# Two fixed small experts open both tracks, in place of one fixed big expert, in a mixture-of-experts block

## The chip, the cores and the metric

The kernel runs on one core of one Trainium2 chip. The metric is the time of one execution on the device in microseconds (us); lower is better. The engines are named as in the profile: PE (matmul) with PEld (its weight loads), DVE (vector), ACT (scalar), POOL, and SP, whose queue issues most DMAs. PEclk is the granted clock of PE, 1.00 being 2.4 GHz and 0.50 being 1.2 GHz.

## The reference, cut to what matters

One layer on 512 tokens of width 1024: a pooling mixer and a latent attention, an output projection, then a mixture of experts with 32 experts, of which each token takes 4, and a final norm. The change touches the experts alone:

```python
logits = (ht @ w_router + b_router).astype(jnp.float32)
top_vals, top_idx = lax.top_k(logits, TOP_K)          # TOP_K = 4 of 32
gates = jax.nn.softmax(top_vals, axis=-1)
...
gu = xblk @ w_gate_up[e] + b_gate_up[e]               # 1024 -> 2048
gate = jnp.minimum(gu[:, :D_EXPERT], SWIGLU_LIMIT)
up = jnp.clip(gu[:, D_EXPERT:], -SWIGLU_LIMIT, SWIGLU_LIMIT)
act = gate * jax.nn.sigmoid(SWIGLU_ALPHA * gate) * (up + 1)
return act @ w_down[e] + b_down[e]                    # 1024 -> 1024
```

All is float32. The weights of an expert are 12 MB: 8 MB for gate and up, 4 MB for down. Router and inputs are fixed by the reference; worked out from it, the experts get 22 to 116 tokens, 12 of them more than 64 (67, 68, 76, 76, 80, 95, 98, 100, 114, 114, 115, 116), and experts 0 and 1 get 58 and 48.

## The kernel before, in words

Until about 200 us the kernel does the attention part, then the second norm and the router. After that it works through 32 positions, one expert each. Which expert stands at a position is decided on the chip: `ordering()` (L1235) ranks the experts by their counts, so that the fullest stand at the big positions. `KINDS` (L40) says what a position is:

- A **big** position (B) holds up to 128 tokens. Its weights are split into two float32r parts (`mhi` on ACT, `mlo` on DVE or POOL, L921 and L922), and each product is three matmuls (`mm3`, L98). 144 matmuls of 128x512 in all: 96 for gate and up, 48 for down.
- A **small** position (S) holds up to 64 tokens and multiplies the float32 weights unsplit, with two 64-column halves of the array side by side. 48 matmuls, each of which the trace shows as two records: 8 records for each MB of weights.

An expert is cut into 12 **items** of 1 MB of weights: gate and up 0 to 7 ("gu"), down 0 to 3 ("dn"). The big experts and the last small one form the x track (results in the psum banks tagged x), the other small ones the y track; `interleave` (L1353) merges both into one `plan` of 384 items, and PE runs it in order. Below, B0gu0 is item gu 0 of the big expert at position 0. Each item has one load of 1 MB into one of 9 slots (`load_slot`, L787), which SP issues in a fixed order; a slot is free again when its item's split or its matmuls are done. A load of an expert that is routed needs the expert's number, `eid` (L1260, read at L1432), which `ordering()` gives. SP also reads `nov` (L1555), the number of experts that overflow their position; it stands in the middle of the loads.

For a routed expert, its tokens are found by `select` (one-hot tiles `oh`, L841 and L843), `slot_info` (matmuls `m<-aux,oh`, L911, and columns `sl`), `fetch` (an indirect DMA of the rows, `xr`, L866) and `gather` (PE transposes `m<-ident,xr`; results in `xgh` and `xgl` for a big expert, in `xgs` for two small ones). After gate and up come the activation, its transposes (`m<-ident,au`), down, and later `combine` (L1106), which adds an expert's rows, or those of a pair of small ones, to `y`.

Position 0 is always expert 0, as a big one: its mask is known early (`mask0`, L658), its rows come straight from matmuls with `oh0` (tile `rows`, L701), its weights need no `eid`, and its eight gate-and-up items run on PE while the routing (`ordering()` and what follows, called by `opening()`, L1485) runs on DVE, PE and ACT. Only then can the first routed expert, S1, start.

Of the kernel before, what the change touches and what calls it, by code (L numbers as in the profile page):

```python
# [39 lines left out]
KINDS = "BSSS" + "BS" * 12 + "SSSS"  # L40
NBIG = KINDS.count("B")

assert len(KINDS) == 32 and KINDS[0] == "B" and KINDS.endswith("SS") and NBIG % 2 == 1
# [7 lines left out]
TURN, SHORT = 0.2, 3.0  # L51
FILL1 = 2
# [70 lines left out]
def block_kernel(ctx: ExitStack, tc: tile.TileContext, xT, x, pos, vecs, w_in, w_pool, w_qb, w_kvb, w_out,  # L123
# [67 lines left out]
    G.memset(keyadd[:, 0:1], BOOST)  # L191
# [46 lines left out]
    dma(br, b_router.partition_broadcast(P))  # L238

# [363 lines left out]
    mask0 = cst.tile([P, NT, 1], BF16, name="mask0")  # L603
    pos0 = cst.tile([P, NT], F32, name="pos0")
# [46 lines left out]
    def choose(a, b, src):  # L651
# [6 lines left out]
        V.tensor_tensor(mask0[:, a:b, :], logits[:, a:b, 0:1], mx[:, a:b, 3:4], op=ALU.is_ge)  # L658
# [27 lines left out]
    def first_slots(tt):  # L686
        a, b = tt[0], tt[-1] + 1
        pw = pt("pw0", bufs=5)
        places(pw, mask0, tt)
        V.scalar_tensor_tensor(pos0[:, a:b], pw[:, a:b], 1.0, mask0[:, a:b, 0], op0=ALU.add, op1=ALU.mult)  # L690
        for t in tt:
            V.tensor_scalar(oh0[:, t, :], iota_s, pos0[:, t:t + 1], None, op0=ALU.is_equal)
# [127 lines left out]
    load_gate_up(0, load_expert(0, 0))  # L820
    load_down(0, wdown[0], range(2))

# [8 lines left out]
    def onx(r):  # L831

        return big(r) or r == E - 1
# [14 lines left out]
    def mate(r):  # L848

        q = next((q for q in range(r + 1, E) if not big(q)), None)  # L850
        return q
# [18 lines left out]
    def gather(r):  # L870
# [66 lines left out]
    def biases(r, cs, first=True):  # L937
        for c in cs:
            bs = bias[:, c * T:(c + 1) * T]
            if big(r):  # L940
                PE.matmul(banks[r][c], lhsT=m4b[0:96, r:r + 1].to_broadcast([96, P]), rhs=bs, start=first,
                          stop=not first)
            else:
                q = 64 * (c % 2)
                PE.matmul(banks[r][c // 2][q:q + 64, :], lhsT=m4b[0:96, r:r + 1].to_broadcast([96, 64]), rhs=bs,
                          start=True, stop=False)

    def gate_up(r, k):


        first = r == 0 or r == "o"
        if k == 0:
            banks[r] = [bank("x" if onx(r) else "y") for _ in range(4 if big(r) else 2)]
        if big(r):
# [4 lines left out]
            for n, (hf, c) in enumerate(todo):  # L959
                cs = slice(c * T, (c + 1) * T)  # L960
                if k == 0 and not first:
                    biases(r, [2 * hf + c])
                mm3(PE, banks[r][2 * hf + c], xg[r][0][:, k, :], xg[r][1][:, k, :], parts[hf][0][:, cs],
                    parts[hf][1][:, cs], first and k == 0, r != 0 and k == KD - 1)
                if n == 1:
                    yield
        else:
            w = wslots.pop((r, "gu", k))
            for c in range(4):
                q = 64 * (c % 2)  # L970
                if k == 0 and c % 2 == 0:
                    biases(r, [c, c + 1])
                PE.matmul(banks[r][c // 2][q:q + 64, :], lhsT=xg[r][:, k, :], rhs=w[:, c * T:(c + 1) * T],
                          start=False, stop=(k == KD - 1))
        if r == 0 and k == KD - 1:
            biases(0, range(4), False)
# [42 lines left out]

    def down(r, j):  # L1020

        if j == 0:
            banks[r] = [bank("x") for _ in range(2)] if big(r) else [bank("y")]
# [26 lines left out]
        else:  # L1050
# [11 lines left out]
            if par == 0:  # L1062
                yb["s"] = (mo.tile([P, 2, T], F32R, tag="ysh", bufs=1, name="ysh"),
                           mo.tile([P, 2, T], F32R, tag="ysl", bufs=1, name="ysl"))
                scat["s"] = [mo.tile([P, T], F32R, tag=f"ss{c}", bufs=1, name=f"ss{c}") for c in range(2)]
            yh, yl = yb["s"]
            places = [(slice(64 * q, 64 * q + 64), q ^ par) for q in range(2)]
            for ps_, c in places:
# [100 lines left out]
    onehot[0] = oh0  # L1169
# [47 lines left out]
    bd = mo.tile([96, D], F32R, tag="ysh", bufs=1, name="bd")  # L1217
    bdraw = [mo.tile([96, T], F32, tag=tag, bufs=n, name="bdraw") for tag, n in (("xgs", 2), ("ats", 1))]
# [10 lines left out]
    gT = mo.tile([96, T], F32R, tag="ss1", bufs=1, name="gT")  # L1229
# [5 lines left out]
    def ordering():  # L1235
# [4 lines left out]
        V.tensor_scalar(keyc, cn[:, E:E + 1], float(E), col(C_KEY), op0=ALU.mult, op1=ALU.add)  # L1240
# [20 lines left out]
        pgp = bank("y")  # L1261
# [5 lines left out]
        pgo = bank("y")  # L1267
# [25 lines left out]
        V.tensor_scalar(capc, rank, float(NBIG), 64.0, op0=ALU.is_lt, op1=ALU.mult)  # L1293
        V.tensor_scalar(capc, capc, 64.0, None, op0=ALU.add)
# [9 lines left out]
        stp = bank("y")  # L1304
# [23 lines left out]
        ovs = bank("y")  # L1328
# [320 lines left out]
```

## Time and profile before

| | |
|---|---|
| time, median of 3 runs (lowest to highest) | 1296.73 us (1294.97 to 1298.3) |
| the profiled execution: its time, its span | 1297.45 us, 1295.4 us |
| mean granted clock of PE | 0.974 |
| busy: PE, DVE, ACT, POOL | 95%, 69%, 44%, 25% |
| a load of 1 MB of gate and up, from issue to landing, median | 9.3 us |
| moved from memory | 430.24 MB, of which 403 MB are the experts' weights |

The span runs from the first to the last instruction; some 2 us of the time lie outside it. Busy shares are averages over stages, and a busy PE may still run at half its clock, so the stretches are read one by one.

### The profile page before, as it was taken

How to read it: one execution, taken by the hardware profiler on the slowest of the kernel's cores; microseconds unless marked ns; L12 is line 12 of the kernel's file. 1: busy time of each engine (PE TensorE's matmuls, PEld its weight loads, DVE VectorE, ACT ScalarE, POOL GpSimd, SP SyncE). 2: the span in 40 equal slices, each digit the busy share in tenths (PEclk: the TensorE clock that was granted, in tenths of full speed). 3: DMA queues.
4: the chain of work that ended last, by engine and by line, in shares of the span. 5: the costliest groups of instructions: out<-in, count | busy, mean ns of one | idle time of the engine just before them, and what ended most of it. 6: DMA issues, size and time to landing. Idle time of an engine off the chain costs nothing.

```text
span 1295.4 us, 16730 instructions
## 1 busy us (share of the span) xinstructions
PE 1230.3 (95%) x5657; PEld 723.6 (56%) x5657; DVE 892.0 (69%) x1568; ACT 571.0 (44%) x819; POOL 319.2 (25%) x262
## 2 busy tenths in 40 slices
PE   7979986799989999999999999999999999999995
PEld 6856765556445555554555555465565555555432
DVE  6897676856767768665776867567677767667424
ACT  5467643444433545443454444345245444443213
POOL 2355452312211122121212113122121312221001
PEclk9999996799999999999999999999999999999998
DMA  8212324889979999999999999999999999999991
GB/s 315 90 50 94 134 82 166 290 319 361 398 318 360 428 415 415 387 405 427 379 408 404 388 384 405 397 367 372 408 406 391 375 425 399 405 424 390 399 406 68
DMA packets 86994, 435.71 MB, mean 336 GB/s; under 512 B 9239, under 2 KB 9239, under 8 KB 54136
## 3 DMA queue, kind: packets, MB, share of 16 engines
q1 hardware_dynamic: 82818, 420.43, 81.1%
q0 software_dynamic: 3888, 13.76, 2.8%
q8 instruction: 46, 0.75, 0.2%
q10 hardware_dynamic: 198, 0.39, 0.1%
q14 instruction: 44, 0.36, 0.1%
HBM read 430.24 MB, written 4.33 MB: 335 GB/s over the span
## 4 chain that ended last, share of the span: by engine, by line
PE 84%; DVE 10%; ACT 2%; issue 2%; DMA 2%; POOL 0%; SPq 0%; DVEq 0%; ACTq 0%; POOLq 0%
PE x L115 32%; PE y L115 30%; PE m L115 11%; PE acc L115 3%; DVE mlo L922 3%; PE po L115 3%; PE s L115 1%; PE pa L115 1%; ACT mhi L921 1%; DMA bdraw<-in_b_down_dram 1%; PE pp L115 1%; DVE oh L843 1%; DMA xr<-hrow,idx 1%; PE rows L115 0%; DVE y L1121 0%
## 5 line engine op out<-in xcount | busy, mean ns | idle before, releaser
L921 ACT CAST mhi<-slot 128x1024 fp32r<-128x1024 f32 x312 | 325.8, 1049 | 283.1 <-PE x L115 247.1
L922 POOL TENSOR_TENSOR mlo<-slot,mhi 128x1024 fp32r<-128x1024 f32 x78 | 193.7, 2483 | 677.3 <-ACT mhi L921 677.2
L922 DVE TENSOR_TENSOR mlo<-slot,mhi 128x1024 fp32r<-128x1024 f32 x234 | 315.4, 1357 | 61.5 <-ACT mhi L921 60.8
L115 PE MATMUL y<-slot,xgs 128*64 128x512 f32 x1152 | 273.1, 604 | 0.0
L1121 DVE TENSOR_TENSOR y<-y,m 128x512 f32<-128x512 f32 x168 | 114.9, 684 | 109.8 <-PE m L115 109.3
L115 PE MATMUL x<-mhi,xgh 128*128 128x512 f32 x416 | 175.8, 429 | 0.0
L115 PE MATMUL x<-mlo,xgh 128*128 128x512 f32 x416 | 166.5, 400 | 3.0 <-DVE mlo L922 2.9
L115 PE MATMUL x<-mhi,xgl 128*128 128x512 f32 x416 | 165.5, 398 | 0.0
L115 PEld LDWEIGHTS y<-slot,xgs 128*64 128x64 f32 x1152 | 75.7, 137 | 132.8 <-issue 130.1
L115 PE MATMUL y<-slot,ats 128*64 128x512 f32 x608 | 144.9, 614 | 0.7 <-ACT ats L1018 0.7
L115 PEld LDWEIGHTS x<-mhi,xgh 128*128 128x128 f32 x416 | 80.3, 194 | 26.1 <-issue 11.6
L115 PEld LDWEIGHTS x<-mlo,xgh 128*128 128x128 f32 x416 | 79.7, 192 | 21.3 <-DVE mlo L922 5.6
L115 PEld LDWEIGHTS x<-mhi,xgl 128*128 128x128 f32 x416 | 79.5, 191 | 17.5
L987 ACT ACTIVATE as<-ag 128x512 f32<-128x512 f32 x45 | 28.4, 631 | 135.9 <-DVE ag L986 135.9
L115 PEld LDWEIGHTS y<-slot,ats 128*64 128x64 f32 x608 | 40.3, 140 | 76.3 <-issue 73.9
L115 PE MATMUL x<-mhi,ath 128*128 128x512 f32 x208 | 68.8, 412 | 0.0
L115 PE MATMUL x<-mhi,atl 128*128 128x512 f32 x208 | 65.7, 397 | 0.0
L115 PE MATMUL x<-mlo,ath 128*128 128x512 f32 x208 | 65.4, 395 | 0.0
L1071 ACT ACTIVATE ysh<-y,sl 64x512 fp32r<-64x512 f32 x36 | 24.6, 684 | 87.5 <-PE y L115 87.3
L1073 DVE SCALAR_TENSOR_TENSOR ysl<-y,sl,ysh 64x512 fp32r<-64x512 f32 x36 | 27.0, 750 | 47.4 <-ACT ysh L1071 46.8
L866 POOL DMA_INDIRECT xr<-hrow,idx x22 | 27.9, 1270 | 88.4 <-DVE idx L863 45.4
L880 DVE SCALAR_TENSOR_TENSOR xgl<-m,gs,xgh 128x128 fp32r<-128x128 f32 x96 | 31.6, 345 | 26.1 <-ACT xgh L879 25.8
(389 smaller groups left out, 1726.6 us busy)
## 6 DMA issues: line engine op xcount, KB each, us to landing
slot<-in_w_gate_up_dram SPq DMA_DIRECT2D x256, 1024.0 KB, 9.3
slot<-in_w_down_dram SPq DMA_DIRECT2D x128, 1024.0 KB, 9.6
wraw<-in_w_in_dram SPq DMA_DIRECT2D x16, 256.0 KB, 4.6
wraw<-in_w_out_dram SPq DMA_DIRECT2D x16, 256.0 KB, 3.4
xtraw<-in_xT_dram SPq DMA_DIRECT2D x8, 256.0 KB, 5.7
y<-in_x_dram SPq DMA_DIRECT2D x4, 512.0 KB, 7.0
hrow<-part POOLq DMA_DIRECT2D x8, 256.0 KB, 2.8
out_dram<-o SPq DMA_DIRECT2D x4, 512.0 KB, 3.5
```

The lines of the kernel that those rows point to most:

```text
L115: r = f(*args, **kwargs)
L843: V.tensor_scalar(oh[:, t, :].rearrange("p (a b) -> p a b", a=2), iota_s[:, 0:64].unsqueeze(1).to_broadcast([P, 2, 64]), src[:, t:t + 1], ...
L866: G.indirect_dma_start(out=rows[r], out_offset=None, in_=hrow, in_offset=bass.IndirectOffsetOnAxis(ap=idx[:, 0:1], axis=0), bounds_check=T ...
L880: V.scalar_tensor_tensor(lo[:, d, :], v, g, hi[:, d, :].bitcast(F32), op0=ALU.mult, op1=ALU.subtract)
L921: S.copy(hi, src)
L922: eng.tensor_tensor(lo, src, hi.bitcast(F32), op=ALU.subtract)
L987: S.activation(sg, g, AF.Sigmoid, scale=1.702)
L1071: S.activation(yh[ps_, c], db[ps_, :], AF.Copy, scale=slots[r][ps_, 6:7])
L1073: V.scalar_tensor_tensor(yl[ps_, c], db[ps_, :], slots[r][ps_, 6:7], yh[ps_, c].bitcast(F32), op0=ALU.mult, op1=ALU.subtract)
L1121: V.tensor_tensor(y[:, t, cs], y[:, t, cs], pb, op=ALU.add)
```

## The change

Positions 0 and 1 are now both small and fixed to experts 0 and 1. Twelve big positions are left, 2, 4, ... 24; twenty are small. Position 0 runs on the x track, position 1 on the y track, so both tracks open with an expert that needs no routing (24 loads without `eid`). `mask0`, `pos0` and `oh0` are made for two experts of 64 tokens; their rows come out of the same matmuls as before, and two DVE operations write them to one `xgs` tile. The bias of these two experts is added at the end of their product. In the plan, `opening()` now prepares positions 2, 3 and 5, and then the slot columns of 0 and 1. `combine` of positions 0 and 1 adds the down bias. The last pair of small ones has only one expert, so the other half of its tiles is filled with zeros. Keys and ranks are adapted.

```diff
-KINDS = "BSSS" + "BS" * 12 + "SSSS"
+KINDS = "SS" + "BS" * 12 + "SSSSSS"
...
+NFIX = 2
+NFREE = 12
...
+    posadd = cst.tile([P, E], F32, name="posadd")
+    G.memset(posadd, 0.0)
+    for r in range(E):
+        if r < NFIX or KINDS[r] == "B":
+            G.memset(posadd[:, r:r + 1], float(-NBIG if r < NFIX else NFIX))
+    G.tensor_tensor(posrank, posrank, posadd, op=ALU.add)
...
         for t in tt:
-            V.tensor_scalar(oh0[:, t, :], iota_s, pos0[:, t:t + 1], None, op0=ALU.is_equal)
+            for e in range(NFIX):
+                V.tensor_scalar(oh0[:, t, 64 * e:64 * e + 64], iota_s[:, 0:64], pos0[:, t, e:e + 1], None,
+                                op0=ALU.is_equal)
...
-    load_gate_up(0, load_expert(0, 0))
-    load_down(0, wdown[0], range(2))
...
-        return big(r) or r == E - 1
+        return big(r) or r == 0 or r == E - 1
...
         if r == 0:
-            for d in range(KD):
-                split_rows(d, rows0[d // 4][:, d % 4 * P:(d % 4 + 1) * P])
+            for b in range(2):
+                V.tensor_tensor(xs[:, 4 * b:4 * b + 4, :], rows0[b].rearrange("p (a b) -> p a b", b=P),
+                                gs[:, 4 * b:4 * b + 4].unsqueeze(2).to_broadcast([P, 4, P]), op=ALU.mult)
             return
...
+            if r == E - 2:
+                for (ps_, c) in places:
+                    other = slice(64 - ps_.start, 128 - ps_.start)
+                    for v in (yh[other, c], yl[other, c], scat["s"][c][other, :]):
+                        V.tensor_scalar(v, iota_t[other, :], 0.0, None, op0=ALU.mult)
...
-    blocks, nx, ny = [tx[:KD]], KD, 0
-    for onx_, run_ in itertools.groupby(interleave(KD, 0, len(tx) - KD // 2)):
+    blocks, nx, ny = [], 0, 0
+    for onx_, run_ in itertools.groupby(interleave(0, 0, len(tx) - KD // 2)):
...
-        if r == 0 and (what == "gu" or k < 2):
-            return
-        if r and r not in wgu:
+        if r < NFIX and r not in wgu:
+            wgu[r] = load_expert(r, r)
+        if r not in wgu:
...
-        yield from arrive(1)
-        yield
-        yield from arrive(bigs[1])
-        yield
-        slot_info(0)
-        yield
+        for g in range(NFIX, NFIX + 2):
+            yield from arrive(g)
+            yield
+        for r in range(NFIX):
+            select(r)
+            yield
+            slot_info(r)
+            yield
         yield from rest
-        yield from gather(1)
-
+
+    queues["rest"].append(opening())
     for i, (what, r, k) in enumerate(plan):
 
-        PE.on = i >= KD
-        if i == 1:
-            queues["rest"].append(opening())
-        while i > 2 and loaded < min(i + 14, len(loads)):
+        PE.on = i >= NFREE
+        while loaded < min(i + (14 if i > 2 else 9), len(loads)):
```

The plan's opening was B0gu0-7, S1gu0-4, B0dn0-3, S1gu5-7, B4gu0-2, S1dn0-3. It is now S0gu0, S1gu0-2, S0gu1-2, S1gu3-4, S0gu3-4, S1gu5-7, S0gu5-7, S1dn0-3, S0dn0-1, S3gu0-1, S0dn2-3, S3gu2-4, B2gu0-1.

On PE, in the opening of the experts, before the change. The rows are the routing's product with `mblk` (it gives `posm`, the tokens' places) and what stands behind it, up to the first slot columns:

```order
L115 MATMUL y<-mblk,pgT 128x64 x4
L115 LDWEIGHTS triu
L115 MATMUL y<-nblkb,triu 32x1
L115 LDWEIGHTS onesb
L115 MATMUL y<-nblkb,onesb 1x1
L115 MATMUL x<-mlo,xgh 128x512
L115 MATMUL x<-mhi,xgl 128x512
L115 MATMUL x<-mlo,xgh 128x512
L115 MATMUL x<-mhi,xgl 128x512
L115 MATMUL x<-mhi,xgh 128x512 x2
```

On PE, at the same place, of the change (line 118 is `mm3` and all other matmuls, as line 115 was):

```order
L118 MATMUL x<-slot,xgs 64x512 x3
L118 MATMUL x<-ident,pg 64x128 x4
L118 MATMUL x<-slot,xgs 64x512 x5
L118 MATMUL y<-slot,xgs 64x512 x8
L118 MATMUL x<-mblk,pgT 128x64 x4
L118 LDWEIGHTS oh
L118 MATMUL m<-aux,oh 128x4
L118 LDWEIGHTS oh
L118 MATMUL m<-aux,oh 128x4
```

Before, 30 matmuls of B0 stood between the product with `mblk` and the first `m<-aux,oh`; now twenty `m<-aux,oh` (five experts, four each) follow at once, and S1gu7 stands behind the last of them.

On DVE, of the change, what these twenty matmuls need, from `posm` on:

```order
L1298 COPY posm<-x 128x128
L1300 TENSOR_SCALAR ga<-x 128x128
L857 TENSOR_SCALAR oh<-iota_s,posm 128x128 x3
L1308 CAST aux<-ga 128x128
L857 TENSOR_SCALAR oh<-iota_s,posm 128x128
L859 TENSOR_SCALAR oh<-iota_s,posm 128x128 x4
L1309 TENSOR_TENSOR aux<-ga,aux 128x128
L929 COPY sl<-m 128x4
```

Before, splits of B0's weights (`mlo`) stood among these operations; now none does, but twelve more `oh` and their columns follow.

On the SP queue, of the change, from the seventh load of the experts' weights on:

```order
L806 DMA slot<-in_w_gate_up_dram 128x2048 x10
L806 DMA slot<-in_w_down_dram 128x2x1024 x6
L1462 TENSOR_LOAD eid
L1462 ISA x2
L806 ISA
L806 DMA slot<-in_w_gate_up_dram 128x2048
L806 ISA
L806 DMA slot<-in_w_gate_up_dram 128x2048
L1579 TENSOR_LOAD nov
```

Before, four loads (two of gu, two of dn) stood there ahead of the first read of `eid`; now sixteen do, and the read of `nov` stands behind load 24 where it stood behind load 14.

## Rows read from the trace of the kernel before

**Rows 1.** The page: granted clock and DMA share in 40 slices, in tenths.

```profile
PEclk9999996799999999999999999999999999999998
DMA  8212324889979999999999999999999999999991
```

**Rows 2.** Windows: engines' busy time (instructions), then PEclk, DMA share, GB/s.

```profile
194.00:226.70 32.70, 22.03 (x135) 17.79 (x134) 21.79 (x64) 9.95 (x18) 9.85 (x16) 0.69 0.45 168
226.70:259.00 32.30, 25.67 (x120) 17.49 (x120) 28.31 (x73) 13.36 (x15) 11.10 (x7) 0.79 0.81 290
400.00:1200.00 800.00, 795.65 (x3622) 448.44 (x3621) 570.96 (x874) 354.63 (x449) 177.81 (x80) 1.00 0.99 399
1040.00:1060.00 20.00, 20.00 (x101) 11.36 (x99) 12.13 (x19) 12.03 (x20) 4.78 (x2) 1.00 1.02 427
```

**Rows 3.** Waits of the SP queue: us in total, times, longest us.

```profile
SPq L787 <- DVE mlo L922: 338.0, 123, 7.6
SPq L787 <- PE y L115: 186.2, 121, 8.0
...
SPq L1432 <- DVE eid L1260: 18.5, 1, 18.5
...
SPq L1555 <- DVE nov L1311: 1.3, 1, 1.3
```

**Rows 4.** Timeline of PE at full clock: start, us, operation.

```profile
711.56 0.39 PE L115 MATMUL x<-mlo,xgh 128*128 128x512 f32 x1
711.79 0.39 PE L115 MATMUL x<-mhi,xgl 128*128 128x512 f32 x1
...
724.94 1.94 PE L115 MATMUL y<-slot,xgs 128*64 128x512 f32 x8
726.81 0.66 PE L115 MATMUL m<-ident,au 128*128 128x128 f32 x4
```

**Rows 5.** Timeline of the opening: start, us, operation [idle before <- releaser].

```profile
199.02 2.66 PE L115 MATMUL rows<-oh,hb 128*128 128x128 f16 x32 [0.55 <-DVE oh L692]
...
206.50 0.19 PE L115 MATMUL m<-mask,triu 128*128 128x32 bf16 x1 [4.82 <-issue]
...
222.06 0.63 PE L115 MATMUL x<-mlo,xgh 128*128 128x512 f32 x1
...
222.08 12.03 SPq L787 DMA_DIRECT2D slot<-in_w_gate_up_dram  x5
...
222.48 0.63 PE L115 MATMUL x<-mhi,xgl 128*128 128x512 f32 x1
...
230.23 0.28 DVE L1272 COPY posm<-y 128x128 f32<-128x128 f32 x1
...
236.50 0.34 PE L115 MATMUL m<-aux,oh 128*128 128x4 f16 x8 [1.29 <-DVE aux L1283]
...
237.57 5.01 SPq L787 DMA_DIRECT2D slot<-in_w_down_dram  x2
...
254.02 1.94 PE L115 MATMUL m<-ident,xr 128*128 128x128 f32 x8 [5.20 <-DMA xr<-hrow,idx]
...
255.15 0.69 DVE L901 TENSOR_TENSOR xgs<-m,gs 128x512 f32<-128x512 f32 x1 [0.41 <-PE m L115]
```

**Rows 6.** Instructions on tile oh, 190 to 260 us: ns min/median/max, first and last start.

```profile
L843 DVE TENSOR_SCALAR oh<-iota_s,posm x12: 266/269/297, 230.8 to 247.9; 128x128 f16<-128x128 f32 x12
```

**Rows 7.** The chain that ended last, just after the opening.

```profile
255.96 7.01 PE y L115 x28
...
270.38 11.39 PE x L115 x48
```

**Rows 8.** Waits of PE, 270 to 400 us: us in total, times, longest us.

```profile
PE m L115 <- DVE xgl L880: 3.8, 1, 3.8
PE m L115 <- DVE au L990: 2.5, 1, 2.5
```

**Rows 9.** Timeline of the end of the last two small experts.

```profile
1265.92 1.51 DVE L1073 SCALAR_TENSOR_TENSOR ysl<-y,sl,ysh 64x512 fp32r<-64x512 f32 x2 [11.89 <-ACT ysh L1071]
```

More of the change, by code (lines that the diff above doesn't have):

```diff
@@ L848, in mate @@
     def mate(r):
-        q = next((q for q in range(r + 1, E) if not big(q)), None)
-        return q
+        return next((q for q in range(r + 1, E) if not big(q)), None)
     rows, nfetch = {}, [0]
@@ L935, in split_item, with fixed, biases @@
         presplit[r, what, k] = out_
-    def biases(r, cs, first=True):
+    def fixed(r):
+        return r != "o" and r < NFIX
+    def biases(r, cs):
         for c in cs:
@@ L940, in biases @@
             if big(r):
-                PE.matmul(banks[r][c], lhsT=m4b[0:96, r:r + 1].to_broadcast([96, P]), rhs=bs, start=first,
-                          stop=not first)
+                PE.matmul(banks[r][c], lhsT=m4b[0:96, r:r + 1].to_broadcast([96, P]), rhs=bs, start=True, stop=False)
             else:
@@ L945, in biases @@
                 PE.matmul(banks[r][c // 2][q:q + 64, :], lhsT=m4b[0:96, r:r + 1].to_broadcast([96, 64]), rhs=bs,
-                          start=True, stop=False)
+                          start=not fixed(r), stop=fixed(r))
     def gate_up(r, k):
-        first = r == 0 or r == "o"
+        first = r == "o"
         if k == 0:
@@ L970, in gate_up @@
                 q = 64 * (c % 2)
-                if k == 0 and c % 2 == 0:
+                if k == 0 and c % 2 == 0 and not fixed(r):
                     biases(r, [c, c + 1])
                 PE.matmul(banks[r][c // 2][q:q + 64, :], lhsT=xg[r][:, k, :], rhs=w[:, c * T:(c + 1) * T],
-                          start=False, stop=(k == KD - 1))
-        if r == 0 and k == KD - 1:
-            biases(0, range(4), False)
+                          start=(k == 0 and fixed(r)), stop=(k == KD - 1 and not fixed(r)))
+                if k == KD - 1 and c % 2 == 1 and fixed(r):
+                    biases(r, [c - 1, c])
     def swiglu(gb, ub, gbias=None, ubias=None):
@@ L1018, in turn @@
                 S.copy(at, tp.rearrange("p (b a s) -> p a b s", b=4, a=2))
+    halfdone = [None]
     def down(r, j):
         if j == 0:
-            banks[r] = [bank("x") for _ in range(2)] if big(r) else [bank("y")]
+            banks[r] = [bank("x") for _ in range(2)] if big(r) else [bank("x" if onx(r) else "y")]
         last = j == KD // 2 - 1
@@ L1346, in items @@
         return [("gu", r, k) for k in range(KD)] + [("dn", r, j) for j in range(KD // 2)]
-    tx = [v for r in range(E) if big(r) or r == E - 1 for v in items(r)]
-    ty = [v for r in range(E) if not big(r) and r < E - 1 for v in items(r)]
+    tx = [v for r in range(E) if onx(r) for v in items(r)]
+    ty = [v for r in range(E) if not onx(r) for v in items(r)]
     def ends_product(v):
@@ L1392, in block_kernel @@
     xorder = [v for v in plan if big(v[1])]
-    loads = xorder[:2]
-    for v in plan:
+    loads = []
+    for i, v in enumerate(plan):
         if not big(v[1]):
             loads.append(v)
+            if v == ("dn", 0, KD // 2 - 1):
+                loads += xorder[:2]
         else:
@@ L1409, in block_kernel @@
     groups = {}
-    for r in range(1, E):
+    for r in range(NFIX, E):
         if big(r):
@@ L1508, in block_kernel @@
             n = xorder.index((what, r, k))
[L1509 to L1511 removed]
+            assert n < nsp
         for g, at in fetch_at.items():
@@ L1534, in block_kernel @@
             step()
-        if big(r) and nsp < len(xorder) and nsp <= n + 2:
-            while nsp < len(xorder) and nsp <= n + 2:
-                split_item(xorder[nsp][1], xorder[nsp][0], xorder[nsp][2])
-                nsp += 1
+        ahead = n + 3 if big(r) else 2 if (what, r, k) == ("dn", 0, KD // 2 - 2) else 0
+        for v in xorder[nsp:ahead]:
+            split_item(v[1], v[0], v[2])
+        nsp = max(nsp, min(ahead, len(xorder)))
         if what == "gu" and k == KD - 1:
-            if r == 0:
-                step(("rest",))
             if r == E - 1:
@@ L1544, in block_kernel @@
             queues["turn x" if onx(r) else "turn y"].append(later(turn(r, act(r)), 3))
-        if what == "dn" and k == KD // 2 - 1:
+        if what == "dn" and k == KD // 2 - 1 and r < E - 2:
             if big(r):
-                queues["rest"].append(later(marked("b", combine([r], r == 0)), 3))
-            elif KINDS[:r + 1].count("S") % 2 == 0 and r != ty[-1][1]:
-                queues["rest"].append(later(marked("s", combine(["s"])), 3))
+                queues["rest"].append(later(marked("b", combine([r])), 3))
+            elif halfdone[0] is None:
+                queues["rest"].append(later(marked("s", combine(["s"], r < NFIX)), 3))
         step()
```

68 lines of the change are left out of this document (35 added, 33 removed).

## The prediction

> **What bounds the kernel now.** I read the page first, then the windows, then the waits and the timeline of the place that stood out. On the page PE is the busiest engine, 95%, and its slices show where it is not at its best: the granted clock is low in slices 7 and 8, just where the experts begin, and DMA becomes full only after them [rows 1]. The windows say the same in numbers [rows 2]. From 400 to 1200 us PE is busy for 795.65 of 800 us at clock 1.00, while DMA moves 399 GB/s. From 194 to 259 us PE is busy for 48 of 65 us, at a clock of 0.69 and 0.79.
>
> Which of PE and DMA leads in the long stretch? DMA is nearly full too, but the SP queue spends 338.0 and 186.2 us waiting for splits and matmuls to give slots back [rows 3], and a 20 us stretch reached 427 GB/s [rows 2]. So the loads follow PE, with some room. PE bounds, and each us of its work or idleness counts one for one.
>
> In the opening PE has too little to cover the routing. After the last matmul of `rows` (199.02 + 2.66 = 201.7) it waits 4.8 us, then runs the routing's first matmuls and B0's gate and up, 22 us of work at full clock, and starts the first routed expert only behind the transposes of 254.02, which waited 5.20 us for `xr` [rows 5]. So of the 54 us from 201.7 to 256 more than half is lost. SP, too, stands 18.5 us for `eid` [rows 3].
>
> **Prices on PE.** At full clock one matmul of a big expert starts 0.23 us after the one before (711.56, 711.79), and an item of a small expert, 8 records, takes 724.94 to 726.81, 1.87 us [rows 4]. So a big expert's matmuls cost 144 x 0.23 = 33.1 us and a small one's 12 x 1.87 = 22.4 us. Bias, slot columns and transposes (a set of four is at most 0.66 us [rows 4]) add some 1.8 us to a small one: 24.2 us. Combines cancel: the additions to `y` are 21 times eight before and after.
>
> **The opening of the change, step by step.** The rows of experts 0 and 1 need two DVE operations of 0.69 us [rows 5] where eight alternations of ACT and DVE stood; the four `oh0` operations become eight, at most 0.3 us apiece. I let PE start S0 at 203.7, two us behind `rows`. Up to S3gu0 it has 22 items (41.1), biases 0.9, four sets of transposes 2, and the routing's own matmuls, some 6 us: 50 us at full clock.
>
> To this come two losses. First, PE restarts cold: at 222.06 and 222.48 a matmul takes 0.42 us in place of 0.23 [rows 5], the 1.2 GHz level, after an idle time just before. I allow 2 us for each restart, as the stretch of [rows 7] lost 2.2 us (below). Second, a hole. The order on PE puts the twenty `m<-aux,oh` directly behind the product with `mblk`, with nothing between them; before, 30 matmuls of B0 stood there and PE waited only 1.29 us [rows 5]. DVE took 6.3 us from `posm` (230.23) to the first eight matmuls (236.50), with splits of B0 in between. Without those, eight one-hots at 0.27 [rows 6] and a few casts make some 3 us for two experts; twelve more one-hots are 3.2 us, their columns 2 to 3: 9 us in all. Bounds: 5 if DVE and PE overlap well, 15 if each round trip between them is paid. I take 9, and a restart behind it. So S3gu0 starts at 203.7 + 50 + 2 + 9 + 2 = 267. Is its `xr` there? From the first slot columns to the transposes of `xr` it took 17.5 us (236.50 to 254.02 [rows 5]). The first slot columns of the change come near 234, so `xr` at 251.5; PE reaches its transposes, behind S1gu7 and S0gu5-7, near 253. It just fits.
>
> **What is left at that moment.** Before, at 255.96: B0's down (11.4 [rows 7], and 1.2 of transposes), 12 big ones, 19 small ones. Of the change, at 267: S0dn2-3 (3.7), 12 big ones, 18 small ones. The difference is 12.6 + 24.2 - 3.7 = 33.1 us. Before also took 14.4 us from 255.96 to 270.38 [rows 7] for five items (9.4), bias and four sets of transposes, 12.2 at full clock: 2.2 us lost, which the 267 already holds for the change.
>
> **Sum:** +11.1 (S3gu0 at 267, not at 255.9) - 33.1 - 2.2 = -24.2 us. The profiled execution took 1297.45 us, 0.7 above the median; so 1296.7 - 24.2, **1272 us**.
>
> **What I cost at nothing.** One big expert fewer takes 24 splits from ACT, DVE and POOL; they wait for PE's slots in the long stretch, not PE for them. The zeros for the half pair are six DVE operations in the 11.89 us for which DVE stands before `ysl` [rows 9]; without that cover they cost some 3 us. `posadd` and `keycol` are used only near 200 us and made at the start. Two waits of PE between 270 and 400 us (3.8 and 2.5 us [rows 8], some 10 with the restarts behind them) come while the tracks are still close together; I leave them in. If they go, the time is 10 us lower; if they double, 10 higher.
>
> **Rivals.**
>
> *The loads set the pace (1282 us).* Two small experts in a row want 12.6 MB each in some 25 us, 500 GB/s, more than the 427 of the fullest stretch [rows 2]. If the end follows the loads, the gain is only what moves earlier. By 256 us before has issued the 10 loads ahead of `eid`, 5 and 2 more [rows 5], and some 3 as slots came free: 20. Of the change, about 17 items used by then and 9 slots make 26. Six loads of 1.05 MB at 399 GB/s are 15.7 us; 1 us less for a pause in the hole: 1282. For it: the share of 0.99 [rows 2]. Against it: SP's waits for slots, and that a big expert, which wants less, follows at once. In a harder form it ends above 1297: the 358 loads that the change has left at 256, 375 MB, would have to move below 373 GB/s (they may take until 35 us before the end, as DMA is idle in the last slice [rows 1]). The 399 GB/s over 800 us speak against that: 0.01.
>
> The Trainium skill has a rule for the harder form: HBM Reference, Specifications, gives a core an effective 358 GB/s, its half of a memory domain, and says that a core alone measures more. By 358 GB/s these loads would take 1049 us and the kernel some 1340. The 399 GB/s of this trace contradict it for a core that runs alone, so the sum doesn't use it.
>
> *SP's queue stops at `nov` (slower, 1301 or more).* The read of `nov` now stands ahead of load 24. `nov` needs a PE product behind S0gu6 and stands on DVE behind S1's activation: near 254 by my count. Load 24, S0dn2, is wanted near 271 and a load takes 9.3 us to land, so some 8 us are to spare; SP's wait now is 1.3 us [rows 3]. Every us beyond stops all loads and then PE. The gain is gone when `nov` is read at 286, and the kernel is slower beyond 290, for which one more late wait of 30 us on DVE would be needed. I see none.
>
> *The gain is larger (1258 us).* The hole is 5 us and the waits of [rows 8] with their restarts go: 4 + 10 below the forecast.
>
> *The change doesn't do what it says.* If expert 0 or 1 had more than 64 tokens, or a thirteenth expert did, an overflow block would run at the end, a big expert with nothing beside it: 12.6 MB at 427 GB/s are 29.5 us, and its last products and combine come on top: 1310 at least. With 58 and 48 tokens, and 12 experts above 64 for 12 big positions, none runs.
>
> **How the numbers follow.** Forecast 0.61, with its own range 1260 to 1283 from the bounds of the hole (-4, +6) and part of the 10 us of the two waits; loads 0.16 (1276 to 1288); larger gain 0.12 (1245 to 1260); `nov` or another new wait that takes the whole gain 0.09, half of it within 0.3%; slower loads and overflow 0.01 each. About 0.3%, 3.9 us, is what a measurement of this kernel can tell from no change. So faster 0.88, same 0.05, slower 0.07. The range leaves out the last two cases and half of the larger gain: 1253 to 1288.
>
> **What would show each step.** Right: `y<-slot,xgs` of a fixed expert near 204; a hole of PE between the product with `mblk` and the last `m<-aux,oh`, near 231 to 240; the first `xr` transposes with at most a short wait; S3gu0 near 267; SP issuing from 205 on without a long pause; clock 1.00 and some 399 GB/s after 400; and the last small expert's down some 24 us earlier. Wrong: PE waiting for a `slot` load in the long stretch (the loads set the pace), SP's wait for `nov` above 8 us, or S3gu0 later than 280.

## The result and the profile after

The changed kernel takes **1267.92 us** (median of 4 runs, 1267.35 to 1269.04) where the kernel before took 1297.38 (4 runs on the same chip, 1294.97 to 1298.3). The medians lie 29.5 us apart; the ratio of the two kernels, with all their runs, is 0.9782, with a 95% interval of 0.9765 to 0.9798. The time is 4 us from the forecast of 1272. The profiled execution took 1268.17 us, with a span of 1266.4.

The page of the changed kernel, which answers to [rows 1] (PE's busy share, granted clock and DMA share in 40 slices, then GB/s):

```profile
PE   7979999899999998999999999999999999999994
PEclk9999999899999998999999999999999999999997
DMA  8312428999999998999998999999999999999981
GB/s 313 100 51 88 146 90 313 409 421 415 416 419 411 404 405 322 360 413 416 402 377 348 420 388 399 402 386 393 381 416 358 361 421 403 377 380 399 422 333 69
```

DMA is full from slice 8 on, two slices earlier than before, and the clock of slices 7 and 8 is 9 and 8, not 6 and 7. But there is a new notch in slice 16: PE at 8, its clock at 8, the transfers at 322 GB/s. The windows of [rows 2] read so now:

```profile
194.00:226.70 32.70, 28.16 (x183) 11.94 (x180) 15.11 (x69) 2.64 (x4) 3.04 (x8) 0.97 0.88 333
226.70:259.00 32.30, 31.31 (x156) 12.37 (x156) 18.57 (x63) 6.62 (x10) 4.04 (x5) 0.91 1.02 412
400.00:1200.00 800.00, 787.23 (x3547) 443.59 (x3547) 556.85 (x826) 347.60 (x441) 173.80 (x77) 0.99 0.97 390
```

In the opening PE is busy for 59.5 of 65 us, at a clock of 0.97 and 0.91. The long stretch is worse than before: 787.23 busy of 800, not 795.65. So something is given back after 400 us.

The opening in the timeline of PE, which answers to [rows 5]:

```profile
198.33 1.94 PE L118 MATMUL x<-slot,xgs 128*64 128x512 f32 x8 [0.34 <-DVE xgs L903]
...
221.74 1.10 PE L118 MATMUL x<-mblk,pgT 64*128 64x64 f32 x8
225.47 0.35 PE L118 MATMUL m<-aux,oh 128*128 128x4 f16 x8 [2.63 <-DVE aux L1309]
226.20 0.45 PE L118 MATMUL m<-aux,oh 128*128 128x4 f16 x2 [0.38 <-DVE oh L859]
226.90 0.38 PE L118 MATMUL m<-aux,oh 128*128 128x4 f16 x2 [0.25 <-DVE oh L859]
227.53 1.74 PE L118 MATMUL m<-aux,oh 128*128 128x4 f16 x8 [0.25 <-DVE oh L859]
229.20 1.98 PE L118 MATMUL y<-slot,xgs 128*64 128x512 f32 x4
...
240.20 0.60 PE L118 MATMUL m<-ident,xr 128*128 128x128 f32 x4
...
254.40 0.39 PE L118 MATMUL y<-bias,m4b 96*64 96x512 bf16 x2
```

S0 starts at 198.33, 0.34 us behind `rows`. The hole is there: from the end of the product with `mblk` (222.84) to 229.20 PE does nothing but the twenty `m<-aux,oh`. The transposes of `xr` start without a wait, and S3gu0 with its bias at 254.40. But they come just behind the fetch that they need, the second of two:

```profile
230.58 1.01 POOL L881 DMA_INDIRECT xr<-hrow,idx  x1 [0.33 <-DVE sl L929]
...
DMA to landing us min/median/max: 8.1/8.5/9.0
```

The first fetch took 8.1 us to land, this one 9.0: it landed at 239.5, some 0.7 us before PE took it.

Two views of the long stretch show what is given back. The waits of PE from 255 us to its end (us in total, times, longest):

```profile
PE m L118 <- DVE xgl L895: 9.2, 4, 4.2
PE m L118 <- DVE au L1008: 1.8, 2, 1.3
PE y L118 <- DVE ysl L1100: 1.2, 1, 1.2
```

The three long ones for `xgl` do not end in the same kind of work. One ends in a combine (`m<-ysh,ss`), one in transposes of activations, one in a set of transposes of gathered rows:

```profile
482.69 0.79 PE L118 MATMUL m<-ysh,ss 128*128 128x512 f32 x1 [4.24 <-DVE xgl L895]
...
644.70 0.66 PE L118 MATMUL m<-ident,au 128*128 128x128 f32 x4 [1.96 <-DVE xgl L895]
...
941.40 0.66 PE L118 MATMUL m<-ident,xr 128*128 128x128 f32 x4 [2.70 <-DVE xgl L895]
```

And windows of 5 us at the four places where the clock falls (PE's busy time, granted clock, DMA share, GB/s):

```profile
479.40:484.40 5.00, 1.71 (x4) 0.73 1.01 423
484.40:489.40 5.00, 5.00 (x15) 0.59 0.85 349
644.40:649.40 5.00, 4.70 (x16) 0.66 0.66 247
939.40:944.40 5.00, 3.00 (x12) 0.81 1.03 424
944.40:949.40 5.00, 5.00 (x20) 0.85 1.02 421
1224.40:1229.40 5.00, 4.32 (x12) 0.66 1.00 370
```

After a wait of 4.24 us at 478 to 482 PE is busy again, but at a mean clock of 0.59. DMA is full during the wait and slower after it: the loads lag behind PE, they don't hold it.

**A ledger.** I added up such windows of 5 us from the first routed item on PE (the bias of S3gu0; before the change, that of S1gu0) to PE's end: idle time is length less busy time, what the clock took is length times (1 - granted clock), and the rest is matmul work at full clock. (The experiments below are in the table too. Each row is one profiled execution; that of gather_alone is the slowest of its five.)

| kernel | first routed item at | from there to PE's end | idle | lost to the clock | rest |
|---|---|---|---|---|---|
| before | 255.89 | 1023.3 | 12.7 | 8.2 | 1002.4 |
| after | 254.40 | 996.0 | 13.5 | 8.5 | 974.0 |
| fewer_loads | 256.80 | 997.0 | 15.8 | 6.8 | 974.4 |
| gather_early | 254.86 | 1001.2 | 20.2 | 8.5 | 972.5 |
| gather_late | 255.87 | 996.3 | 15.8 | 5.1 | 975.4 |
| gather_alone | 256.54 | 991.3 | 9.5 | 6.8 | 975.0 |
| alone_six | 256.90 | 984.1 | 9.0 | 1.7 | 973.4 |
| early_splits | 269.59 | 991.7 | 13.5 | 3.4 | 974.8 |
| free_thirteen | 260.81 | 991.8 | 13.5 | 3.4 | 974.8 |

The rest is the same within 3 us in every kernel with this order of experts. So the difference of the two kernels is 1.5 us at the first routed item, 28.4 of work, and 1.1 lost again to idle time and clock: 28.8 of the 29.0 us between the spans.

The column of the clock is the least steady. After, early_splits and free_thirteen have the same order on PE behind S3gu0 and the same waits there, yet lost 8.5, 3.4 and 3.4 us to the clock. Behind the wait of 1.96 us the clock fell to 0.66 in after (the window at 644.40 above); behind the same wait early_splits kept it:

```profile
658.50:663.50 5.00, 4.69 (x24) 2.37 (x26) 3.98 (x7) 4.58 (x9) 2.39 (x1) 1.00 0.62 231
```

So some 5 us of this column can differ between executions of one order.

### The profile page after: what moved, and what is told of

It reads as the page before. It is cut to its first block, busy times and chain, and to the rows that moved or that the text cites. A ratio compares the mean times of both kernels' runs of the same rounds, so it can differ in the third digit from the quotient of the medians.

```text
span 1266.4 us, 16525 instructions
## 1 busy us (share of the span) xinstructions
PE 1213.0 (96%) x5597; PEld 697.3 (55%) x5597; DVE 865.4 (68%) x1552; ACT 542.7 (43%) x785; POOL 303.7 (24%) x272
## 4 chain that ended last, share of the span: by engine, by line
PE 74%; DVE 7%; DMA 1%; issue 1%; ACT 1%; POOL 0%; DVEq 0%; ACTq 0%; POOLq 0%
PE x L118 33%; PE y L118 29%; PE m L118 11%; DVE mlo L938 3%; DMA bdraw<-in_b_down_dram 1%; DVE au L1007 1%; ACT mhi L937 1%; DVE oh L859 0%; DVE au L1008 0%; DVE ag L1004 0%; DVE au L1006 0%; DVE xgl L895 0%; DVE ss L1096 0%; DVE y L1130 0%; DVE o L1186 0%
## 5 line engine op out<-in xcount | busy, mean ns | idle before, releaser
L937 ACT CAST mhi<-slot 128x1024 fp32r<-128x1024 f32 x288 | 300.6, 1049 | 260.9 <-PE x L118 236.1
L938 DVE TENSOR_TENSOR mlo<-slot,mhi 128x1024 fp32r<-128x1024 f32 x216 | 288.3, 1347 | 66.3 <-ACT mhi L937 65.8
L938 POOL TENSOR_TENSOR mlo<-slot,mhi 128x1024 fp32r<-128x1024 f32 x72 | 177.4, 2464 | 642.5 <-ACT mhi L937 642.4
L118 PE MATMUL x<-mhi,xgh 128*128 128x512 f32 x384 | 164.0, 427 | 0.0
L118 PE MATMUL x<-mlo,xgh 128*128 128x512 f32 x384 | 152.0, 396 | 0.1
L118 PE MATMUL x<-mhi,xgl 128*128 128x512 f32 x384 | 151.4, 394 | 0.0
L118 PEld LDWEIGHTS x<-mhi,xgh 128*128 128x128 f32 x384 | 72.7, 189 | 25.7 <-issue 12.2
L118 PEld LDWEIGHTS x<-mhi,xgl 128*128 128x128 f32 x384 | 72.1, 188 | 17.0
L118 PEld LDWEIGHTS x<-mlo,xgh 128*128 128x128 f32 x384 | 72.4, 189 | 15.9 <-DVE mlo L938 1.1
L881 POOL DMA_INDIRECT xr<-hrow,idx x21 | 28.7, 1367 | 94.5 <-DVE idx L878 48.7
L894 ACT ACTIVATE xgh<-m,gs 128x128 fp32r<-128x128 f32 x96 | 33.4, 366 | 31.9 <-PE m L118 16.7
```

The costliest lines, as they stand in the source:

```text
L118: r = f(*args, **kwargs)
L881: G.indirect_dma_start(out=rows[r], out_offset=None, in_=hrow, in_offset=bass.IndirectOffsetOnAxis(ap=idx[:, 0:1], axis=0), bounds_check=T ...
L894: S.activation(hi[:, d, :], v, AF.Copy, scale=g)
L937: S.copy(hi, src)
L938: eng.tensor_tensor(lo, src, hi.bitcast(F32), op=ALU.subtract)
```

## The experiments

The theory: PE bounds, so the kernel follows PE's work, its idle time and its clock; the two fixed experts keep PE at work while the routing is found. The main rival: the loads set the pace. A second: what is won or lost at one place comes back at the next wait.

### Does PE or the transfers set the pace? (two_more_big, fewer_loads)

```diff
-KINDS = "SS" + "BS" * 12 + "SSSSSS"
+KINDS = "SS" + "BS" * 14 + "SS"
```

> Two of the twenty small positions become big ones again (fourteen big, eighteen small), after the opening; the loads are the same 384, all of the same size, and the opening is untouched. Theory (PE bounds the long stretch): on PE 288 matmuls at 0.23 us come in (66.2), 24 items of 1.87 us go (44.9), one combine of 16 matmuls (3.7) and four sets of transposes (2.2) come in: +27 us, 1295, within 5 us for waits that fall elsewhere. Rival (the loads set the pace): nothing, 1268 to 1272, as no byte more is moved.

Measured: 1307.13 us (ratio to before 1.0077, 1.0053 to 1.0100), 39 us more than after. The rival with 0 falls: no byte more is moved. But it is 12 us more than the theory had. The ledger from the start of S0 on (after: 1052.0 us to PE's end, this kernel: 1090.8) has 32.1 us more work at full clock, 11.4 more idle time and 4.9 less lost to the clock. So the work is 5 us more than I had counted, and the rest is idle time, most of it at one new place:

```profile
PE m L118 <- DVE atl L1033: 10.7, 8, 1.3
```

I read this as a big expert that costs PE its matmuls and also moves where the splits fall on DVE; no run here shows the second part by itself. These eight waits are short (1.3 us at most), and the clock hardly falls behind them.

```diff
-        if what == "gu":
+        if what == "gu" and k % 2 and r in (9, 13, 17, 21):
+            wslots[r, "gu", k] = wslots[r, "gu", k - 1]
+        elif what == "gu":
             load_gate_up(r, wgu[r], [k])
```

> For the big experts at positions 8, 12, 16 and 20 by name 9, 13, 17 and 21 (small ones where the position is odd) the odd row blocks of gate and up are not loaded; the products take the block before a second time. So 16 loads of 1.05 MB, 16.8 MB, are left out, and those rows of the weights with them; PE, ACT, DVE and POOL do the same work. Theory (PE bounds): no change beyond 3 us either way. Rival (the loads set the pace): 16.8 MB at 399 GB/s, 42 us less, 1226.

(The four positions, 9, 13, 17 and 21, are small experts; the first words of the expectation name the big ones beside them.) Measured: 1270.23 us (0.9790, 0.9769 to 0.9812). With 4% fewer bytes the time is the same or 2 us longer, where the rival had 42 less. The same window as above, of this kernel:

```profile
400.00:1200.00 800.00, 784.86 (x3542) 443.16 (x3540) 559.18 (x826) 349.15 (x442) 174.34 (x77) 0.99 0.93 369
```

The transfers go from 390 to 369 GB/s and PE is not busier for it. PE bounds.

### Is it the early loads that fill the opening? (fixed_waits)

```diff
-        if r < NFIX and r not in wgu:
+        if r < 1 and r not in wgu:
             wgu[r] = load_expert(r, r)
...
-        while loaded < min(i + (14 if i > 2 else 9), len(loads)):
+        while loaded < min(i + (14 if i > 2 else 9), len(loads)) and (i or loads[loaded][1] < 1):
```

> Of the two fixed experts only 0 stays fixed for the loads: those of expert 1 read its number from eid, as those of a routed expert do, and S0's twelve loads are issued ahead of them. The scheduler also orders some matmuls of the attention part otherwise, so the comparison goes from the end of rows on. Theory (the gain in the opening is that PE has two experts to run while the routing is worked out): S1's items can't start before eid (215.5) and a landing of some 9 us, near 226, so PE stands or has S0 alone from 198 on: 10 to 20 us slower, 1278 to 1288. Rival (the gain is the one big expert fewer, and cover in the opening counts little): within 3 us of 1268.

Measured: 1293.0 us (0.9973, 0.9962 to 0.9984). The edit did more than I meant: SP's program put the read of `eid` ahead of all loads but the first, so S0's waited too. The waits of SP, then the timelines of SP and PE:

```profile
SPq L1462 <- DVE over L1324: 50.3, 1, 50.3
```

```profile
207.59 2.61 SPq L806 DMA_DIRECT2D slot<-in_w_gate_up_dram  x5
```

```profile
228.84 1.94 PE L118 MATMUL y<-slot,xgs 128*64 128x512 f32 x8 [0.55 <-DMA slot<-in_w_gate_up_dram]
231.34 1.94 PE L118 MATMUL x<-slot,xgs 128*64 128x512 f32 x8 [0.56 <-DMA slot<-in_w_gate_up_dram]
233.82 1.94 PE L118 MATMUL x<-slot,xgs 128*64 128x512 f32 x8 [0.55 <-DMA slot<-in_w_gate_up_dram]
```

`rows` ends at 198.48, as in after, and `eid` is read near 207. From 224 us on PE does an item each 2.48 us, not each 1.87: one load of 1.05 MB, 423 GB/s. Here the loads do set the pace, as the rival said of two small experts in a row. S3gu0 comes at 269.11, 14.7 us later than after, and another 8.4 us are lost behind it (idle time 21.6). So 25 us hang on the loads being issued before the routing is known, where I had expected 10 to 20 for those of S1 alone. The same small experts, with the same kinds of positions, win little without that: 4 us on the kernel before.

### What were the 3.7 us by which `rows` came earlier? (early_splits)

```diff
     queues["rest"].append(opening())
+    for what, r, k in loads[:2]:
+        load(what, r, k)
+        loaded += 1
+        for hf in range(2):
+            split(wslots[r, what, k][:, hf * D:(hf + 1) * D], V)
```

> The four splits that ACT and DVE did for B0 before the change, near 154 to 162 us, come back: the first two loaded row blocks are split once more, and nobody reads the result. Theory: they hold up y on DVE, PE waits some 3 us for it and restarts cold, rows ends 3 to 4 us later, and the whole kernel is 3 to 4 us slower (1271 to 1272). Rival: rows came earlier for another reason, or the opening has slack behind it: within 1 us of 1268.

The kernel before at 166 to 170 us, a stretch that was not shown above, then early_splits, on PE; the changed kernel has the same transposes at 166.15 without a wait:

```profile
169.48 0.44 PE L115 MATMUL tp<-ident,y 128*128 128x128 f32 x2 [2.98 <-DVE y L544]
169.67 0.64 PE L115 MATMUL po<-whi,mixh 128*128 128x512 f32 x1
170.11 0.63 PE L115 MATMUL po<-wlo,mixh 128*128 128x512 f32 x1
```

```profile
168.71 0.44 PE L118 MATMUL tp<-ident,y 128*128 128x128 f32 x2 [1.98 <-DVE y L559]
```

In the kernel before, DVE is at two splits of B0 from 157.25 to 162.29, and `y` comes late; PE waits 2.98 us and goes on at half its clock (0.43 us a matmul). The four splits bring 1.98 us of the wait back, and the last 32 matmuls of `rows` start at 198.62, against 196.05 of after and 195.2 to 196.5 of the other kernels with an unchanged attention part; they end at 200.57. The median is 1271.09 us (0.9803, 0.9784 to 0.9823), 3.2 more than after; the intervals of the two ratios overlap, so the time alone hardly shows it, but the wait in the trace does.

### What is the hole worth, and does `xr` just fit? (free_eight, free_thirteen, free_fourteen)

One number is changed, which sets up to which item the scheduler may order PE as it likes: 8 in free_eight, as shown, 13 in free_thirteen, 14 in free_fourteen.

```diff
-NFREE = 12
+NFREE = 8
```

> NFREE is 8 in place of 12, so that the order on PE puts the items S0gu5 and S1gu6 between the five sets of slot columns: twelve of the twenty m<-aux,oh stay directly behind the product with mblk. Theory (PE's idle time in the opening counts one for one, and the fetch of xr has some us to spare): the wait of 2.6 us for aux stays, that of the last eight goes, so 1 to 2 us less, 1266 to 1267. Rival (what is won in the opening is given back at the next wait): within 0.5 us of 1268, or slower by the 3.7 us that the fetch for the first big expert comes later.

> NFREE is 13: the order on PE puts the second half of S1gu7 with its biases, some 2 us, between the product with mblk and the twenty m<-aux,oh; nothing moves on DVE. Theory (the hole of 6.4 us is DVE's time from posm to aux and its one-hots; work put into it costs nothing and keeps PE busy): the wait of 2.6 us for aux shrinks below 1, S3gu0 comes some 2 us sooner after the start of S0 (54 in place of 56.1), 1265 to 1266.5. Rival (the stretch is set by the fetch of xr or by DVE, not by PE): S3gu0 comes no sooner, 1268, with a new wait for xr.

> NFREE is 14: S1gu7's second half and S0gu5 to S0gu7, some 9 us, stand ahead of the twenty m<-aux,oh. Theory (xr just fits: it landed near 238 to 240, and PE took it at 240.2): the hole goes, but idx, the fetch and xr come some 8 us later and PE has used up what covered them: a wait of 6 to 10 us for xr, S3gu0 1 to 5 us later after S0 than 56.1, 1269 to 1273. Rival (the fetch has room, the hole is what counts): S3gu0 comes 5 to 6 us sooner, 1262.

Measured: 1270.92 us (0.9803, 0.9776 to 0.9829), 1270.76 (0.9802, 0.9781 to 0.9823) and 1281.83 (0.9882, 0.9861 to 0.9902). None is faster. The three traces say why.

free_eight: from the end of the product with `mblk` (218.48) to the next item (222.85) it is 4.4 us, not 6.4, but PE also waits 0.87 ahead of that product, and behind the hole it goes on at half its clock, as in after: sixteen records take 6.28 us, where 3.65 is full clock. From S0 to S3gu0 it takes 57.0 us, of them 4.5 idle and 4.1 lost to the clock; after took 56.1, with 4.2 and 3.4. The rival is nearer.

free_thirteen: the 2 us of S1gu7 went where I wanted them, but with S1gu7 done its activation became ready, and DVE took it ahead of `aux`. DVE in after (first two lines) and in free_thirteen:

```profile
222.88 0.29 DVE L1298 COPY posm<-x 128x128 f32<-128x128 f32 x1 [6.50 <-PE x L118]
...
224.98 0.43 DVE L1309 TENSOR_TENSOR aux<-ga,aux 128x128 f16<-128x128 f32 x1
```

```profile
224.24 0.29 DVE L1298 COPY posm<-x 128x128 f32<-128x128 f32 x1 [7.36 <-PE x L118]
...
224.64 0.68 DVE L1004 TENSOR_SCALAR ag<-y 128x512 f32<-128x512 f32 x1
...
226.94 0.68 DVE L1006 TENSOR_SCALAR au<-y 128x512 f32<-128x512 f32 x1
227.54 0.43 DVE L1309 TENSOR_TENSOR aux<-ga,aux 128x128 f16<-128x128 f32 x1
```

From `posm` to `aux` it is now 3.3 us, not 2.1. The wait for `aux` is 2.42 all the same, and a new one of 2.13 us stands at `xr`. S3gu0 comes 62.1 us after S0, where I had expected 54 and after had 56.1. This execution is only 2 us longer than that of after all the same, as it lost 5 us less to the clock behind S3gu0 (see the ledger). In free_fourteen the wait for `xr` is most of the story; the two kernels' waits:

```profile
243.88 1.09 PE L118 MATMUL m<-ident,xr 128*128 128x128 f32 x4 [2.13 <-DMA xr<-hrow,idx]
...
249.59 1.09 PE L118 MATMUL m<-ident,xr 128*128 128x128 f32 x4 [11.09 <-DMA xr<-hrow,idx]
```

The fetch comes as late as the one-hots do, and nothing is left to cover it: S3gu0 68.2 us after S0 and the kernel 13.9 us slower than after, where I had expected 1 to 5 and a wait of 6 to 10. So `xr` just fits in the changed kernel, with the 0.7 us read above, and in these runs items that PE needs later as cover did not fill the hole with profit.

### The waits of the long stretch (gather_first, gather_early, gather_late, gather_alone, alone_six)

```diff
             if drain and name not in drain:
                 continue
+            if name == "rest" and not drain and queues["gather"] and r > 3:
+                continue
```

> While a gather has a set of transposes to go, no combine is worked on (from position 4 on), so that the two m banks are not shared by both. Theory (the four waits of PE for xgl, 9.2 us, come from a combine that wants the bank which the gather still holds, and cold restarts follow them): they go, 9 to 14 us less, 1254 to 1259. Rival (PE waits wherever DVE is behind, and a wait removed comes back as another): within 3 us of 1268, with the idle time listed under au, atl or ysl.

Measured: 1268.93 us (0.9791, 0.9768 to 0.9814). The theory fell in this form: `PE m <- DVE xgl` is 9.1 us in four, as in after. Two of the three long ones end in transposes, which this edit does not hold back.

gather_early and gather_late change only the item at which a gather begins (`firsts(g) - 8` and `- 6` from position 5 on, in place of `- 7`).

> The transposes and splits of gathered rows are begun eight items ahead of their expert, not seven (from position 5 on). Theory (the waits are a matter of where the gather falls against the combines, the work is the same): PE's idle time behind S3gu0, 13.3 us now, changes, and the time follows it one for one, with up to as much again for cold restarts: the wait for xgl shrinks by half or more, 1258 to 1265. Rival (idle time there is made up later, or the loads follow on): within 2 us of 1268 whatever the idle time is.

> The same begun six items ahead (from position 5 on). Theory (time follows PE's idle time): the splits of a big expert are nearer to their first use, so waits of PE for xgl or xgh are as long or longer, 1268 to 1275, and the time differs from 1268 by what the idle time behind S3gu0 differs from 13.3 us, times one to two. Rival: within 2 us of 1268 whatever the idle time is.

Measured: 1274.61 us (0.9833, 0.9810 to 0.9855) and 1271.33 (0.9808, 0.9779 to 0.9836). My guess of the sign for gather_early was wrong: the wait for `xgl` grows to 14.3 us. That the time follows the idle time holds here: 6.7 us more of it than after, 6.7 us more time. gather_late has 2.3 us more idle time and loses 3.4 less to the clock; behind S3gu0 it takes as long as after, and the rest of its 3.4 us lies ahead of it and in the spread of its runs (1268.5 to 1273.4).

What remained was a finer form of the theory, for the wait that does end in a combine: it asks for an `m` bank right behind the second set of transposes, while ACT and DVE still split both sets. On top of gather_first, in `gather()` of a big expert:

```diff
+                if b and r != "o":
+                    yield
+                    yield
+                    yield
```

> As gather_first, and the gather of a big expert keeps the combine away for three steps more (some 4 us of products on PE) after its second set of transposes. Theory (PE waits for xgl because a combine asks for an m bank right behind the second set of transposes, and the eight splits on ACT and DVE have not given one back): the waits for xgl (9.1 us in four) fall below 4, idle time behind S3gu0 from 13.3 to some 6 to 8, and the time by that or, with the restarts, some more: 1258 to 1263. Rival (the bank is wanted next by a set of transposes of the activations, or DVE is late anyway): the idle time stays at 11 or more, under au or xgl, and the time within 3 us of 1268.

Measured: 1260.82 us (0.9726, 0.9704 to 0.9748), 7 us faster than after. The waits are not gone, but smaller (9.5 us idle, where I had expected 6 to 8):

```profile
PE m L118 <- DVE xgl L895: 5.2, 3, 3.0
```

The combine still waits 2.96 us, the transposes of activations 1.96; the wait of 2.70 in the gathered rows is gone. So the theory holds in part: one of the waits is of the kind that it names, and another went as the order shifted.

The last kernel waits six steps and takes a cast off ACT.

```diff
                 if b and r != "o":
-                    yield
-                    yield
-                    yield
+                    for _ in range(6):
+                        yield
...
-            S.copy(bd[:, cs], bdraw[c])
+            G.tensor_copy(bd[:, cs], bdraw[c])
```

> Two edits on gather_alone. The combine is kept away for six steps after a big gather, not three. And the cast of bd runs on POOL in place of ACT, where it waited for the bdraw transfer ahead of the exponential of the routing (ex at 211.0). Theory: the wait of 2.96 us for xgl near 488 goes with its restart, 3 to 5 us; ex comes at 208 to 209, but PE has products of S0 and S1 until 221.7 all the same, so the routing gains nothing from it: 1256 to 1258. Rivals: the combine, held longer, comes late for the next one that needs its tiles and PE waits for y, ysl or ybl instead (1261 or more); or the earlier routing shortens the opening too (1254 to 1256, S3gu0 sooner than 56.1 after S0).

Measured: **1257.74 us** (0.9697, 0.9683 to 0.9710), 10 us faster than after and 39 faster than before. Its waits behind 255 us, and the long window:

```profile
PE m L118 <- DVE au L1011: 3.5, 2, 2.3
PE m L118 <- DVE xgl L895: 2.2, 2, 2.0
...
400.00:1200.00 800.00, 791.70 (x3592) 446.57 (x3592) 557.36 (x829) 348.40 (x442) 172.70 (x77) 1.00 0.99 396
```

The combine's wait is gone, the one of 1.96 us stays, and a new one of 2.3 us for `au` has come. By the ledger it has only 0.5 us less idle time than gather_alone, but loses 1.7 us to the clock, not 6.8: its waits are shorter, and only one of them is followed by a slow stretch. That row overstates the step, as the two executions are 6.9 us apart and the medians 3.1. The exponential of the routing runs at 209.10, not 211.02 as in after; but with the cast still on ACT it ran at 209.36 in gather_alone, so the cast on POOL is not shown to have moved it. From S0 to S3gu0 it is 56.9 us, no shorter.

## Why the prediction was right, and where its sizes were off

The mechanism held: PE bounds, the opening is where it stood, and the fixed experts fill it. Step by step:

- **PE starts S0 at 203.7.** Measured 198.33. The start was mis-sized by 5.4 us: 3.7 because `rows` ends at 198.0, not 201.7, and 1.7 because S0 follows it at once. The first part was missed outright: B0's four early splits on ACT and DVE went with B0, and I had costed splits only in the long stretch. early_splits puts 2 to 3 us of it there. The rest is the clock of that execution: in ten other kernels with the same program up to there, `rows` ends between 198.3 and 200.1.
- **The hole, 9 us.** Measured 6.4, inside the bounds of 5 and 15. Its place in PE's order and its cause, DVE's `aux` and one-hots, were as forecast; of the 6.4 us 3.8 are idle and 1.8 lost to the clock.
- **Two restarts, 4 us, and 50 us of work at full clock.** By windows of 5 us the 56.1 us from S0 to S3gu0 are 4.2 idle, 3.5 lost to the clock and 48.4 of work. There is one restart, behind the hole; at the start of S0 the clock did not fall in the profiled execution.
- **S3gu0 at 267.** Measured 254.40, so +11.1 became -1.5: 12.6 us better than the sum had it, 5.4 from the start and the rest from the hole, the missing restart and 1.5 us less work.
- **`xr` just fits.** Right, with 0.7 us to spare, though 13 us earlier than I had it: the fetch began sooner because the one-hots did.
- **33.1 us less work behind S3gu0.** Measured 28.4 by the ledger. By the counts of both programs, with the prices of [rows 4], it should be some 33. The 4 to 5 us between stay open, as do the 5 us by which two_more_big has more work than counted: each is 0.5% of the matmul time of that stretch.
- **Before's own loss of 2.2, and two waits left in.** In the trace of before idle time and clock took 2.7 us of the stretch up to 270.38, and 9.7 from there to 400, so both sizes were nearly right. Both went with the change, which loses nothing before 400 us; the waits behind 400 us took their place, 22.0 us against 8.4. Over the whole stretch it is 20.9 us before and 22.0 after. That the sum stayed was luck, not mechanism: gather_early and alone_six move it from 28.7 down to 10.7 by small shifts in the order.
- **`nov` and the loads.** `nov` is read at 238 without a wait, and PE waits for no `slot` load behind the opening. SP still waits 334.6 and 193.9 us for slots, as in [rows 3].

So two terms were off by much and in opposite directions: the opening by 12.6 us to the good, work and losses behind it by 7.9 to the bad (35.3 forecast, 27.4 measured). Their difference, 4.7 us, is most of the 5.1 between 1273.25 (1297.45 - 24.2, the forecast on the profiled execution's own base) and 1268.2. That the time came so near to the forecast is in part luck: each of the two errors is larger than what is left of them.

**The rivals.** The loads set the pace: shown wrong for the long stretch by fewer_loads, and shown right for a row of small experts without loads in advance by fixed_waits. Eight of the loads are issued before `rows` ends, and PE never waits for one in the change. The larger gain, 1258 us, asked for a hole of 5 us and for the waits of [rows 8] to go: they went, but others came, and alone_six reaches that time by other edits. That the slower harder form does not come is seen on the page: the transfers move 409 to 421 GB/s in slices 8 to 13. The Trainium skill (HBM Reference, Specifications) has 358 GB/s for a core's share and says that a lone core measures more; this trace agrees with the second half.

## What to carry to other kernels

Look for what a removed step kept busy ahead of its own place, not only at it: four splits in another stage had cost PE a wait of 3 us. Price an idle stretch of PE as a range: in these traces the matmuls behind it often ran at half clock for a while, and the same waits (13.5 us in all) cost 3.4 us more in two executions and 8.5 in another. When you put work into a hole, follow what that work makes ready: it will queue on the engine that the hole was waiting for.

## What the runs showed of the hardware

The landing of a small transfer on the ACT queue varies widely. The `bdraw` loads were issued at 195.1 to 197.2 in the changed kernel while SP's prefetch ran; the second landed after some 14 us, and ACT stood in front of it with the exponential of the routing behind it:

```profile
195.13 2.11 ACTq L1303 DMA_DIRECT2D bdraw<-in_b_down_dram  x2
...
210.50 0.62 ACT L1249 CAST bd<-bdraw 96x512 fp32r<-96x512 f32 x1 [7.91 <-DMA bdraw<-in_b_down_dram]
211.02 0.21 ACT L1232 ACTIVATE ex<-ex 128x16 f32<-128x16 f32 x1
```

In the profiled execution of early_splits, the slowest of its six at 1279.11 us, the same cast ran only at 222.70, some 22 us after the issue, and PE waited 9.64 us for what hangs on it. Its other runs took 1270 to 1273. In two_more_big, with the same prefetch beside it, it was 7.7 us; in fixed_waits, where SP issued no load between 156 and 207 us, 7.2; in the kernel before, with two loads of 1 MB beside it, 11.1. So the full queues are a likely cause of the long cases, but no run isolates it. The time of that landing is not the same from run to run, so in a kernel like this one an engine that works in order should not wait for it ahead of the critical chain.

After 4.24 us without work at 478 us PE's matmuls came 0.43 us apart for 6 us, then 0.23 again. The last 32 matmuls of `rows` took 1.95 us in some executions and 3.57 in others, with the same order on PE and nearly the same wait ahead of them (0.68 to 1.01 us): the granted clock, not the program, makes differences of 1.6 us there. The same holds for what a wait costs behind it: of the seven waits above 0.5 us that after, early_splits and free_thirteen share behind S3gu0, four were followed by a lower clock in after (4.24, 1.96, 2.70 and 0.68 us), and only the two longest in the others.
